# Moving six of sixteen small copies from SyncE's DMA queue to ScalarE's, in the first attention pair of an encoder block

## The chip, the cores and the metric

The kernel runs on one core of a Trainium2 chip. The metric is the device time of one execution in microseconds (us). A core has five engines that run their own instruction streams and wait for each other by semaphores: TensorE (PE in the profile) for matmuls, VectorE (DVE), ScalarE (ACT), GpSimd (POOL) and SyncE (SP). SP, ACT and POOL can also issue DMA transfers; in this kernel SP issues nearly all of them.

## The reference

Two layers on a 512 x 1024 float32 input. Layer A is dilated sliding-window attention, layer B a 2-D neighbourhood attention. Cut to layer A's core:

```
hn   = rms_norm(x)
proj = hn @ w_in                       # q, k, v of three dilation groups, and a gate
for g, dilation in ((0, 1), (1, 4), (2, 16)):
    q, k = rms_norm(q_g), rms_norm(k_g)          # per head, 16 heads of 64
    logits = q @ k.T * scale + t5_bias           # only keys within the window
    p = exp(logits - max); denom = sum(p)
    out_g, lse_g = (p @ v) / denom, max + log(denom)
y = sum over g of softmax(lse)_g * out_g         # merged by denominators
x = x + (y * silu(gate)) @ w_out
```

## The kernel before, in words

Layer A works on its 16 heads in eight pairs, `hc` 0 to 7. All large products are done in three passes of float32r halves (`mm3`: high by high, high by low, low by high), so each weight block that comes from memory (`wraw`) is first cast by ACT to its high half (`wh`, in `cast`, L157) and then subtracted by POOL or DVE to its low half (`wl`, in `rest`, L162). Casts run five to six weight blocks ahead of the matmuls that use them.

TensorE's order is written by hand. Two generators are interleaved: `main` (L1378) yields after each `mm3` of the large products; `side` (L1390) holds the attention of the pair that was projected last. `run` (L1142) steps `main` and, in between, lets `side` go on when a planned time is over. That time is `clock`, which only `matmul` and `transpose` move (L320 to L328): a step of `mm3` on 512 columns counts 640 units. `later_on(delay, job)` (L344) writes a job of another engine at the first step whose clock has passed the delay; `yield "wait", key, delay` holds `side` until `stamp[key]` plus the delay. These numbers set the order in which instructions are written, for PE, and from the first pair on also for the other engines, whose instructions of layer A are kept in program order; on the chip each waits only for its semaphores.

The attention of a pair is `attn_a` (L938). `scores(u)`, twice, writes the logits of two tiles of 128 queries by two heads. For each of these four, `least` adds the bias and takes the minimum on DVE, `exponents` and `normalise` run on ACT, and `turn` transposes the 128 x 512 block of probabilities in 32 x 32 blocks on DVE into `pq` (shown as `pt`). For the two dilated groups `pq` is then in place. For the undilated group the 32-row blocks have to change partitions: `move(n)` (L954) copies, for four (n, b), 32 partitions x 512 elements (64 KB) from `pq` to `t0` (also shown as `pt`) by DMA: sixteen copies for a pair. When all are written, `stamp["pt", hc]` is set.

Then `v_a` (L789) transposes the values `vt` on PE (`tp`) and copies them with ACT to `v`; `weigh` (L1037) multiplies probabilities by values into four `o` banks: two groups of 64 matmuls on `pq` and `rawk`, then 64 on `t0` and `v`, with steps of the large products in between; `weighed` (L851) multiplies the gate `gt` by `o` on DVE. The next pair's bias `e` is loaded by `bias_a` (L874) from SP, six loads; in the first pair behind `weigh`, in later ones ahead of it. Meanwhile `main` ends the pair's own projection: `v0_a(0)` (L673) with its `vt` copies on ACT, then the last product (`put21`, L724, whose squares of `rawk` run on ACT), and the next pair's first product.

In the first pair the sixteen moves are written on SP at delays 8000, 9300, 10600 and 11900 behind the second scores, four at a time.

Of the kernel before, what the change touches and what calls it, by code (L numbers as in the profile page):

```python
# [26 lines left out]
NHC = 8  # L27
# [19 lines left out]
def tile_hybrid_encoder(  # L47
# [49 lines left out]
    vec, act, pol, syn = (Ordered(e) for e in (nc.vector, nc.scalar, nc.gpsimd, nc.sync))  # L97
# [246 lines left out]
    def later_on(delay, job):  # L344

        timers.append((clock[0] + delay, job))
        timers.sort(key=lambda t: t[0])
# [441 lines left out]
    def v_a(hc):  # L789

        yield "wait", ("vt", hc), 2500
        vt = st.pop(("vt", hc))
        tp = bank("tp")
        for i in range(4):
            transpose(tp[:, i * P : (i + 1) * P], vt[:, i * P : (i + 1) * P])
        st["v0"] = wk.tile([P, 2, 4, P], F32, tag="k12", name="v0", bufs=1)[:, 0]
        act.copy(st["v0"], tp.rearrange("p (i c) -> p i c", i=4))
        yield
# [75 lines left out]
    def bias_a(hc):  # L874
        e0 = wk.tile([P, 2, 256], F32, tag="e0", name="e0", bufs=1)
        e12 = wk.tile([P, 4, 224], F32, tag="e12", name="e12", bufs=1)
        for hd in range(2):
            h = 2 * hc + hd
            syn.dma_start(
                e0[:, hd, :],  # L880
                bass.AP(l0_d.tensor, l0_d.offset + h * 1600 + 127, [[400, 4], [-4, 32], [1, 256]]),
            )
            for g in range(2):
                syn.dma_start(
                    e12[:, 2 * hd + g, :],
                    bass.AP(l12_d.tensor, l12_d.offset + h * 512 + 256 * g + 31, [[0, 4], [-1, 32], [1, 224]]),
                )
        return e0, e12
# [49 lines left out]
    def attn_a(hc):  # L938
# [6 lines left out]
        moved = []  # L945
# [5 lines left out]
            src = pr[:, 512 - P * n : 512]  # L951
            vec.transpose(dst, src.rearrange("p (i b k) -> p i b k", b=4, k=32))

        def move(n):  # L954

            place = t0.rearrange("p (a x) -> p a x", a=4)
            for b in range(4):
                a = (b + n) % 4
                src = pq[32 * a : 32 * a + 32, 1024 * b : 1024 * b + 512]
                tc.keep_in_program_order(syn.dma_start(place[32 * b : 32 * b + 32, a, :], src))  # L960
            moved.append(n)
            if len(moved) == 4:
                stamp["pt", hc] = clock[0]

        def scores(u):

            tiles = []
            for t in (2 * u, 2 * u + 1):
                cs, n = (64, 192) if t == 0 else (0, 192) if t == 3 else (0, 256)
                tiles.append((t, [bank("log") for _ in range(2)], cs, n))  # L970
            for t, lgs, cs, n in tiles:
                ks = slice(P * t + cs, P * t + cs + n)
                qs = slice(P * t, P * t + P)
                mm3_heads(
                    [lg[:, cs : cs + n] for lg in lgs],
                    lambda hs: q0h[hs, qs], lambda hs: q0l[hs, qs],
                    lambda hs: k0h[hs, ks], lambda hs: k0l[hs, ks], False,
                )
            for t, lgs, cs, n in tiles:
                for g in range(2):  # L980
                    for j in range(4):
                        c = P * t + 32 * j
                        for hd in range(2):
                            hs = slice(64 * hd, 64 * hd + 64)
                            matmul(
                                lgs[hd][32 * j : 32 * j + 32, 256 + P * g : 384 + P * g],
                                q12[hs, g, c : c + 32],
                                by_class(k12[hs, g, :])[:, :, j],
                                share=2,
                                start=False,  # L990
                                stop=(g == 1),
                            )
            return [(hd, t, lgs[hd], cs, n) for t, lgs, cs, n in tiles for hd in range(2)]
# [68 lines left out]
        if last:  # L1062
# [21 lines left out]
            for c in range(4):  # L1084
                src = gt.rearrange("p (t ja x) -> p x ja t", t=4, ja=8)[:, 4 * c : 4 * c + 4]
# [15 lines left out]
        for u in range(2):  # L1101
            for n, tile_ in enumerate(scores(u)):
                later_on(400 + 900 * n, partial(least, n, tile_))
            if u:
                stamp["scored", hc] = 0
                for n in range(4):
                    later_on(8000 + (2000 if hc else 1300) * n, partial(move, n))
            yield 8500
        fill = bias_rows() if hc == 2 else None
        yield from v_a(hc)  # L1110
        yield "wait", ("pt", hc), 2500
        if hc:
            st["e", hc + 1] = bias_a(hc + 1)
        yield "wait", ("pt", hc), (4500, 11500)[hc] if hc < 2 else 9000 if hc == NHC - 2 else 7500
        yield "wait", ("gate", hc), 4000
        gt = weighed(hc, (yield from weigh()))
        if not hc:
# [272 lines left out]
    def side():  # L1390
# [17 lines left out]
        for hc in range(NHC):  # L1408
            yield from k_a(hc)
            yield from attn_a(hc)  # L1410
# [109 lines left out]
```

## Time and profile before

| | us |
|---|---|
| Median of three runs | 858.39 |
| Lowest and highest | 854.2 and 860.99 |
| The profiled execution | 856.92 |
| Its span, first to last instruction | 855.1 |

The page of the profile gives the engines' busy time and the costliest groups; further views of the same trace list instructions in order of time (start, length, engine, line, operation, output and inputs, and in brackets the idle time ahead of it with what ended it), waits, the chain of work that ended last, the rows of one tile, and busy time by stretch. Nearly all rows have L85 or L324, the lines of the helpers that record an operation and a matmul, so rows are told apart by tile names. SPq, ACTq and POOLq are DMA issues. A wait for several semaphores is put down to the one that came last by the trace.

### The profile page before, as it was taken

Reading aid. Unit: us, or ns where it says so; the run is one execution under the profiler, and the core shown is the slowest. Engines: PE = TensorE matmul, PEld = TensorE weight load, DVE = VectorE, ACT = ScalarE, POOL = GpSimd, SP = SyncE. Lnnn points to the kernel's source line nnn. Section 1 sums busy time; section 2 is a strip of 40 time slices with the busy share of each in tenths; the row PEclk is TensorE's granted clock in tenths of the full one; section 3 lists DMA queues with packets and bytes.
Section 4 is the critical chain, followed back from the end, with each engine's and each line's share of the span. In section 5 each row is a group of like instructions: output and inputs, shape, how many; then the busy total and the mean of one; then the engine's idle time right before and its main releaser. Section 6 shows DMA issues by size and latency. Waiting matters only on the chain.

```text
span 855.1 us, 18125 instructions
## 1 busy us (share of the span) xinstructions
PE 833.6 (97%) x6611; PEld 688.8 (81%) x6611; DVE 634.5 (74%) x1653; ACT 507.5 (59%) x1066; POOL 296.5 (35%) x259
## 2 busy tenths in 40 slices
PE   9998989999999999999999999899999999999998
PEld 6876867878877878878877877689998898889786
DVE  7899895797897787786886866656578666776742
ACT  7566665765855846846846828545456654665440
POOL 5045442362453543543533514113123322322301
PEclk9999999999999999999999999999999999999999
DMA  9425754766676775776675664283264456534212
GB/s 339 138 56 134 206 130 136 144 164 193 136 174 193 159 176 180 161 164 184 157 174 178 126 193 144 80 297 112 81 193 145 124 169 185 158 134 126 84 50 99
DMA packets 56169, 131.97 MB, mean 154 GB/s; under 512 B 7184, under 2 KB 24528, under 8 KB 55952
## 3 DMA queue, kind: packets, MB, share of 16 engines
q1 hardware_dynamic: 49744, 108.78, 40.5%
q0 software_dynamic: 6048, 22.02, 15.0%
q8 instruction: 52, 0.85, 0.4%
q14 instruction: 37, 0.30, 0.1%
q10 hardware_dynamic: 288, 0.01, 0.0%
HBM read 111.73 MB, written 11.72 MB: 144 GB/s over the span
## 4 chain that ended last, share of the span: by engine, by line
PE 70%; ACT 10%; DVE 10%; DMA 5%; issue 3%; SPq 1%; POOL 1%; ACTq 0%; DVEq 0%
PE acc L324 58%; ACT p L85 4%; PE log L324 4%; PE o L324 4%; DMA wraw<-in_w 3%; PE tp L328 3%; DVE wl L85 2%; ACT wh L85 2%; SPq L85 1%; ACT rawk L85 1%; DVE rawq L85 1%; DVE na L85 1%; DMA e<-l_d 1%; DVE p L85 1%; DVE gt L85 1%
## 5 line engine op out<-in xcount | busy, mean ns | idle before, releaser
L85 POOL TENSOR_TENSOR wl<-wraw,wh 128x512 fp32r<-128x512 f32 (+1 forms) x153 | 197.4, 1291 | 425.2 <-PE acc L324 200.2
L85 ACT CAST wh<-wraw 128x512 fp32r<-128x512 f32 (+1 forms) x360 | 209.7, 593 | 198.9 <-PE acc L324 158.2
L85 DVE TENSOR_TENSOR wl<-wraw,wh 128x512 fp32r<-128x512 f32 (+1 forms) x207 | 160.4, 778 | 43.3 <-PE acc L324 33.9
L324 PE MATMUL acc<-wh,hn_h 128*128 128x384 f32 (+1 forms) x488 | 186.7, 383 | 3.0 <-DVE gt L85 1.7
L324 PE MATMUL acc<-wl,hn_h 128*128 128x384 f32 (+1 forms) x488 | 177.5, 364 | 0.4 <-DVE wl L85 0.4
L324 PE MATMUL acc<-wh,hn_l 128*128 128x384 f32 (+1 forms) x488 | 177.5, 364 | 0.0
L85 ACT ACTIVATE p<-p,mn 128x256 f32<-128x256 f32 (+2 forms) x248 | 137.7, 584 | 32.1 <-DVE mn L85 32.1
L324 PEld LDWEIGHTS acc<-wh,hn_h 128*128 128x128 f32 x488 | 92.3, 189 | 21.6 <-issue 6.8
L324 PEld LDWEIGHTS acc<-wh,hn_l 128*128 128x128 f32 x488 | 92.1, 189 | 9.8
L324 PEld LDWEIGHTS acc<-wl,hn_h 128*128 128x128 f32 x488 | 92.6, 190 | 8.5 <-DVE wl L85 1.1
L324 PE MATMUL acc<-wl,mix_h 128*128 128x512 f32 x224 | 88.2, 394 | 2.1 <-DVE wl L85 2.1
L324 PE MATMUL acc<-wh,mix_h 128*128 128x512 f32 x224 | 89.5, 400 | 0.0
L324 PE MATMUL acc<-wh,mix_l 128*128 128x512 f32 x224 | 87.8, 392 | 0.0
L324 PE MATMUL acc<-hn_h,wh 128*128 128x512 f32 x192 | 79.0, 412 | 0.3 <-ACT rawb L85 0.2
L324 PE MATMUL acc<-hn_h,wl 128*128 128x512 f32 x192 | 75.1, 391 | 0.0
L324 PE MATMUL acc<-hn_l,wh 128*128 128x512 f32 x192 | 75.0, 391 | 0.0
L85 DVE STREAM_TRANSPOSE pt<-p 128x512 f32<-128x512 f32 (+1 forms) x60 | 40.6, 687 | 23.7 <-ACT p L85 23.6
L85 DVE TENSOR_REDUCE ss<-sq 128x4 f32<-128x256 f32 (+1 forms) x96 | 46.1, 500 | 11.1 <-POOL sq L85 5.9
L324 PE MATMUL acc<-y_h,wh 128*128 128x512 f32 x128 | 51.9, 405 | 0.5 <-ACT gt L85 0.5
L324 PEld LDWEIGHTS acc<-wl,mix_h 128*128 128x128 f32 x224 | 42.3, 189 | 11.5 <-DVE wl L85 3.3
L324 PEld LDWEIGHTS acc<-wh,mix_h 128*128 128x128 f32 x224 | 42.2, 188 | 10.0 <-issue 1.6
L324 PE MATMUL acc<-y_h,wl 128*128 128x512 f32 x128 | 50.0, 391 | 0.0
(149 smaller groups left out, 1379.8 us busy)
## 6 DMA issues: line engine op xcount, KB each, us to landing
wraw<-in_w SPq DMA_DIRECT2D x95, 512.0 KB
wraw<-in_w POOLq DMA_DIRECT2D x42, 512.0 KB, 7.0
wraw<-in_w SPq DMA_DIRECT2D x38, 384.0 KB
pt<-pt SPq DMA_DIRECT2D x112, 64.0 KB
td<-tr SPq DMA_DIRECT2D x24, 224.0 KB
pt<-td SPq DMA_DIRECT2D x24, 224.0 KB
e<-l_d SPq DMA_DIRECT2D x32, 112.0 KB
e<-l_d SPq DMA_DIRECT2D x16, 128.0 KB
```

The source lines that it names most:

```text
L85: m = f(*args, **kw)
L324: nc.tensor.matmul(o, l, r, **kw)
L328: nc.tensor.transpose(o, i, ident)
```

## The change

In the first pair (`hc` 0), ten of the sixteen moves stay on SP's queue and six are issued on ACT's. The six are single moves, written one by one at delays 12000 to 16500; the ten on SP are written at 8000, 9000, 10000 and 11000. The stamp is set when all sixteen are written, so the two waits behind it, 2500 and 4500 before, are 0 in the first pair. The other pairs keep their sixteen moves on SP, their delays and their waits.

```diff
-        def move(n):
+        def move(n, queue, bs):
 
             place = t0.rearrange("p (a x) -> p a x", a=4)
-            for b in range(4):
+            for b in bs:
                 a = (b + n) % 4
                 src = pq[32 * a : 32 * a + 32, 1024 * b : 1024 * b + 512]
-                tc.keep_in_program_order(syn.dma_start(place[32 * b : 32 * b + 32, a, :], src))
-            moved.append(n)
-            if len(moved) == 4:
+                tc.keep_in_program_order(queue.dma_start(place[32 * b : 32 * b + 32, a, :], src))
+                moved.append(a)
+            if len(moved) == 16:
                 stamp["pt", hc] = clock[0]
+
+        def moves():
+            if hc:
+                for n in range(4):
+                    later_on(8000 + 2000 * n, partial(move, n, syn, range(4)))
+                return
+            for n in range(4):
+                later_on(8000 + 1000 * n, partial(move, n, syn, (0, 2, 3) if n % 2 else (1, 3)))
+            for i, (n, b) in enumerate(((0, 0), (0, 2), (1, 1), (2, 0), (2, 2), (3, 1))):
+                later_on(12000 + 900 * i, partial(move, n, act, (b,)))
...
             if u:
                 stamp["scored", hc] = 0
-                for n in range(4):
-                    later_on(8000 + (2000 if hc else 1300) * n, partial(move, n))
+                moves()
...
-        yield "wait", ("pt", hc), 2500
+        yield "wait", ("pt", hc), 2500 if hc else 0
         if hc:
             st["e", hc + 1] = bias_a(hc + 1)
-        yield "wait", ("pt", hc), (4500, 11500)[hc] if hc < 2 else 9000 if hc == NHC - 2 else 7500
+        yield "wait", ("pt", hc), (0, 11500)[hc] if hc < 2 else 9000 if hc == NHC - 2 else 7500
```

## The prediction

> **What bounds the kernel now.** I read the page's head first, to see which engine has no slack, then the waits of the stretch that the edit touches.
>
> ```profile
> span 855.1 us, 18125 instructions
> PE 833.6 (97%) x6611; PEld 688.8 (81%) x6611; DVE 634.5 (74%) x1653; ACT 507.5 (59%) x1066; POOL 296.5 (35%) x259
> PE o L324 <- DMA e<-l_d: 2.8, 1, 2.8
> PE o L324 <- DMA pt<-pt: 1.0, 1, 1.0
> ```
>
> PE is busy for 97%, so only its idle time and its slow matmuls are to be had. The waits of 104 to 134 us put 3.8 us of idle PE ahead of the matmuls into `o`, on DMAs. The first is put down to `e<-l_d`, but those matmuls read `pt` and `v` and no `e`: a shared landing, misread. PE's timeline there, and the same group in the next pair, where nothing waits:
>
> ```profile
> 125.28 0.39 PE L324 MATMUL acc<-wh,hn_l 128*128 128x512 f32 x1
> 128.50 0.59 PE L324 MATMUL o<-pt,v 128*64 128x64 f32 x8 [2.83 <-DMA e<-l_d]
> 130.06 3.06 PE L324 MATMUL o<-pt,v 128*64 128x64 f32 x56 [0.97 <-DMA pt<-pt]
> 133.06 0.80 PE L324 MATMUL acc<-wh,hn_h 128*128 128x512 f32 x1
> 193.56 2.08 PE L324 MATMUL o<-pt,v 128*64 128x64 f32 x64
> 195.57 0.50 PE L324 MATMUL acc<-wh,hn_h 128*128 128x512 f32 x1
> ```
>
> PE runs dry at 125.67 (125.28 + 0.39) and is back on `acc` at 133.06: 7.39 us. In the next pair the same 64 matmuls take 2.01 (193.56 to 195.57). So the stall costs 5.4 us here, of which 3.8 is idle and 1.6 slow matmuls (the granted clock below). What it waits for, by the chain, by SP's timeline and by the rows of `pt`:
>
> ```profile
> 112.77 0.70 DVE L85 STREAM_TRANSPOSE pt<-p 128x512 f32<-128x512 f32 x1
> 113.50 11.74 SPq L85 DMA_DIRECT2D pt<-pt  x16
> L85 SPq DMA_DIRECT2D pt<-pt x16: 515/591/1458, 113.5 to 124.6; - x16
> 124.63 5.39 DMA pt<-pt
> 125.36 0.50 SPq L85 DMA_DIRECT2D wraw<-in_w  x1
> 125.91 6.67 SPq L85 DMA_DIRECT2D e<-l_d  x6
> ```
>
> The last transpose ends at 113.47; SP issues 16 moves one after another until 125.24 (11.74/16 = 0.73 us each); the sixteenth starts at 124.63 and has landed 5.39 us later, at 130.02, when PE goes on. Is SP's issuing the limit, or the transfer? DMA by stretches of 2 us (length, granted clock, share, GB/s):
>
> ```profile
> 116.00:118.00 2.00, 1.00 0.43 106
> 118.00:120.00 2.00, 1.00 0.32 80
> 122.00:124.00 2.00, 1.00 0.81 131
> 126.00:128.00 2.00, 1.00 1.06 223
> 130.00:132.00 2.00, 0.58 0.50 189
> 132.00:134.00 2.00, 0.56 0.20 55
> ```
>
> While SP issues moves alone, the DMA engines are a third busy: the issue is the limit. Only from 122 do they fill, with POOL's accumulating loads, `wraw` and `e`. The last two rows show the clock halved just behind the stall.
>
> **The change, part by part.** *Moved, not removed:* the same 16 transfers of 64 KB; six issue on ACT, ten stay on SP. Order from the code: the planner counts 640 units for three matmuls. The six fire at 12160, 13440, 14080, 14720, 15796 and 17076; the copy of `vt` is written at 12160, just behind the first. `weigh` was due at 17076 and, with the waits now zero behind the last move, is due there again: PE's order does not change.
>
> *SP:* ten moves at 0.73 us from 113.50 end at 120.8 (at 0.63, the usual spacing without its two long ones, 119.8). Its last starts near 120.1; with the same 5.39 us it has landed by 125.5. Behind it the `wraw` load and six `e` loads go out some 4.5 us earlier; `e` is free (its readers are the minima of the scores) and nobody waits for it before the next scores.
>
> *ACT:* what its queue holds there:
>
> ```profile
> 113.49 0.60 ACT L85 CAST wh<-wraw 128x512 fp32r<-128x512 f32 x1
> 114.00 1.05 ACT L85 COPY vt<-acc 128x512 f32<-128x512 f32 x1
> 115.08 0.24 ACT L85 COPY vt<-vt 128x64 f32<-128x64 f32 x1
> 116.28 0.58 ACT L85 COPY v<-tp 128x512 f32<-128x512 f32 x1
> 116.75 1.33 ACT L85 CAST wh<-wraw 128x512 fp32r<-128x512 f32 x2
> 124.04 0.42 ACT L85 ACTIVATE sq<-rawk 128x256 f32<-128x256 f32 x1 [5.96 <-DVE rawk L85]
> 0.74 0.41 ACTq L85 DMA_DIRECT2D ng<-in_norm_gain  x1
> 1.18 0.46 ACTq L85 DMA_DIRECT2D hg<-in_head_gain  x1
> 1.18 4.10 DMA hg<-in_head_gain
> 115.38 0.65 PE L328 MATMUL tp<-ident,vt 128*128 128x128 f32 x4 [0.24 <-ACT vt L85]
> ```
>
> The wait for the last transpose (113.47) is over when ACT arrives at 114.0, so the first move adds no wait, only its issue. Price of one issue on ACT: no row shows a move there. Nearest below, 0.41 (`ng` at 0.74); above, SP's longest move, 1.46; I take SP's median, 0.59, the same transfer. Six cost 3.5 us (2.5 to 8.8). ACT was idle for 5.96 us from 118.08 to 124.04, so 3.5 is hidden: its last move starts near 121.0 and is out by 121.6. Queued behind the moves are four casts of `wh`, up to 3.5 us late; who waits for them:
>
> ```profile
> 121.26 1.59 POOL L85 TENSOR_TENSOR wl<-wraw,wh 128x512 fp32r<-128x512 f32 x1
> 124.53 0.68 DVE L85 TENSOR_TENSOR wl<-wraw,wh 128x512 fp32r<-128x512 f32 x1
> ```
>
> These two subtract the last two casts (casts are used in order), at 121.26 and 124.53, and the casts would end by 119.9 and 121.0: hidden. If an issue cost 1.46, the last cast would end near 125.2, still ahead of its matmuls at 129.7, but the sixth move would not start before 125.4.
>
> What isn't hidden: the first move stands ahead of the `vt` copy, and PE already waits 0.24 us for that copy ahead of `tp`. **Price: one issue, +0.6** (bounds: 0, if ACT's sequencer issues while the cast at 113.49 still runs; 1.46).
>
> *The landing:* PE now comes to the last 64 matmuls at 126.3 (125.67 + 0.6). The sixth ACT move starts at 121.0; from issue to landing the rows give 4.10 (`hg`, on this queue) and 5.39 (above), and the page's median for POOL's 512 KB loads is 7.0:
>
> ```profile
> wraw<-in_w POOLq DMA_DIRECT2D x42, 512.0 KB, 7.0
> ```
>
> That is 125.1, 126.4 or 128.0: a wait of 0 to 1.7 us, by the middle row 0.1. I take 0.1, since 5.39 was measured on a move in full DMA engines, which it will meet again.
>
> *Rules weighed.* The Trainium skill, "DMA: Bandwidth & Descriptors", section "Issuing engines are not separate DMA queues", says that several issuing engines share the same 16 DMA engines and save only the initiating time, usually small beside the transfer. The shares of 0.32 and 0.43 above speak for issue as the limit; by the rule the landing stays at 130 and the sum is 0 (rival B, from rows).
>
> *What is late next.* DVE multiplies `gt` by `o` after its own chain, and PE's next transposes need the banks that this frees:
>
> ```profile
> 130.54 0.42 DVE L85 TENSOR_TENSOR rawk<-rawk,rs 128x256 f32<-128x256 f32 x1
> 132.54 0.93 DVE L85 TENSOR_TENSOR gt<-gt,o 128x128 f32<-128x128 f32 x4 [1.58 <-PE o L324]
> 136.91 0.60 PE L328 MATMUL tp<-ident,rawq 128*128 128x128 f32 x4
> 133.00:194.00 61.00, 60.81 (x542) 48.79 (x540) 47.29 (x112) 40.54 (x79) 26.95 (x22) 0.99 0.63 145
> ```
>
> With `o` done at 128.4, DVE comes to it at 130.96 and frees the first bank at 131.2; PE reaches `tp` at 128.4 + 3.5 = 131.9. That fits by 0.7 us. Behind 133 PE is busy for 60.81 of 61 us (first number after the length), so what is saved is passed on.
>
> *Sum:* −5.4 (stall and slow matmuls) −0.3 (the first `acc` step took 0.80 us at the low clock, 0.50 in the next pair) +0.6 +0.1 = **−5.0 us**. The profiled execution took 856.92 (span 855.1): it becomes 851.9. The median of the three runs is 858.39, 1.5 above: 853.4 there, which I give.
>
> **The rivals.**
>
> *A, part of the wait stays.* `wraw` and `e` are pulled forward into the landing of ACT's moves, beside POOL's loads. With the 7.0 us landing PE waits 1.7 instead of 0.1, and at the upper issue price a little more: −2 to −3.4, about 855.7 on the median. For: the share of 1.06 at 126. Against: ACT's moves stand on a queue of their own, not behind SP's. Whether so short a wait halves the clock too, no row here shows; I price it without. The rows of 130 to 134 show the clock halved behind 3.8 us of idle; the Trainium skill, "TensorE: Matmul & The Clock Gate", section "Part 1: The HAM clock gate", gives an idle window of about 3.4 us as what throttles it, which agrees, and by which 1.7 us would cost only itself.
>
> *B, nothing saved: the transfer is the limit, or the change doesn't do what it says.* Either the moves land no earlier, or the sixth falls behind the square of `rawk`, which stood until 124.04. It would start at 124.5, land at 129.9, and PE goes on at 130.06 as before; the 0.6 ahead of `tp` only shortens the wait. That is 858.4, no change. Against: the shares, and the planner's 17076 for the move, 800 ahead of the square.
>
> *C, slower: ACT's issue is dear.* It decides from about 1.4 us for each. ACT then ends its sixth move at about 126.9 (118.08 + 8.8), started at 125.4, landed at 130.8; PE loses 1.46 ahead of `tp`, comes at 127.1, waits 3.7, and goes on at 130.8 instead of 130.06, at the low clock: +0.7, and six times the excess of whatever an issue takes beyond 1.46: 859.1, 860 at 1.6. For: SP has such rows (1458 ns). Against: its median is 591.
>
> **Chances and range.** The forecast 0.62, A 0.18, B 0.12, C 0.05; 0.03 for a knock-on later in the kernel, of either sign. Runs before spread from 854.2 to 860.99, so 1% (8.6 us) is about what a measurement here tells from no change. The whole stall is 5.7 us, 0.66%: faster by over 1% needs luck or a knock-on, 0.08; slower by over 1% 0.03; within, 0.89. Range: from no loss ahead of `tp` with a low median (−7, and the spread of the runs), 848.5, to C at 860, which takes in B.
>
> **What would show it.** Right: ten moves on SP, gone by 121; six on ACT between 113.5 and 121.6 at about 0.6 each; `tp` from `vt` idle for about 0.8; the last 64 matmuls at about 126.3, within 2.1 us, at a clock of 1.00 from 130 to 134; `gt` times `o` at 131. Wrong: an idle PE ahead of these matmuls of over 2 us (A, B), an ACT issue over 1.2 (C), a sixth move behind the square (B), or a new wait behind 133 that takes the gain back.

## The result, and the profile after

The changed kernel took 850.86 us (median of 8 runs, 849.09 to 852.54) against 858.38 for the kernel before beside it (8 runs): a ratio of 0.9923 [0.9896, 0.995]. That is −7.5 us. A second comparison gave 851.66 against 856.49: 0.9945 [0.9929, 0.996], or −4.8 us. The forecast was −5.0 us. Both ratios are less than 1% below 1, and neither interval takes in 1. The profiled execution took 849.09 us, with a span of 847.1.

The head of the page, then SP's timeline and PE's around the last 64 matmuls (start, length, engine, line, operation, output and inputs, idle time ahead):

```profile
span 847.1 us, 18124 instructions
PE 828.3 (98%) x6611; PEld 684.4 (81%) x6611; DVE 634.2 (75%) x1653; ACT 507.8 (60%) x1066; POOL 297.4 (35%) x259
```

```profile
112.66 6.77 SPq L85 DMA_DIRECT2D pt<-pt  x10
119.56 0.50 SPq L85 DMA_DIRECT2D wraw<-in_w  x1
120.10 10.63 SPq L85 DMA_DIRECT2D e<-l_d  x6
...
114.71 0.65 PE L328 MATMUL tp<-ident,vt 128*128 128x128 f32 x4 [0.86 <-ACT vt L85]
...
124.53 0.39 PE L324 MATMUL acc<-wh,hn_l 128*128 128x512 f32 x1
124.85 2.08 PE L324 MATMUL o<-pt,v 128*64 128x64 f32 x64
126.87 0.50 PE L324 MATMUL acc<-wh,hn_h 128*128 128x512 f32 x1
...
130.41 0.60 PE L328 MATMUL tp<-ident,rawq 128*128 128x128 f32 x4
```

The 64 matmuls stand in one row now, of 2.08 us, with no idle time in brackets; before they were two rows with 2.83 and 0.97 ahead. From the end of the last `acc` step (124.92) to the next (126.87) PE spends 1.95 us, where it spent 7.39. Ten moves leave SP in 6.77 us. The other six, on ACT's timeline, stand between its casts (`wh`) and copies in the order of the working (some rows are left out at the dots, here as elsewhere):

```profile
112.66 0.61 ACT L85 CAST wh<-wraw 128x512 fp32r<-128x512 f32 x1
112.67 0.61 ACTq L85 DMA_DIRECT2D pt<-pt  x1
113.32 1.06 ACT L85 COPY vt<-acc 128x512 f32<-128x512 f32 x1
...
114.42 0.51 ACTq L85 DMA_DIRECT2D pt<-pt  x1
...
116.99 0.78 ACTq L85 DMA_DIRECT2D pt<-pt  x1
117.28 0.62 ACT L85 CAST wh<-wraw 128x512 fp32r<-128x512 f32 x1
123.14 0.42 ACT L85 ACTIVATE sq<-rawk 128x256 f32<-128x256 f32 x1 [5.24 <-DVE rawk L85]
```

The rows of the tile `pt` give the issues (lowest, median and highest length in ns, first and last start):

```profile
L85 SPq DMA_DIRECT2D pt<-pt x10: 523/590/666, 112.7 to 118.8; - x10
L85 ACTq DMA_DIRECT2D pt<-pt x6: 514/579/779, 112.7 to 117.0; - x6
```

The DMA view of 112 to 119 says which packets of ACT's queue, q10, began there (packets, MB, share of the engines):

```profile
q10 hardware_dynamic: 288, 0.39, 23.3%
```

And two stretches (start and end, length, busy time of PE, PEld, DVE, ACT and POOL, granted clock, DMA share, GB/s):

```profile
126.00:128.00 2.00, 2.00 (x38) 1.76 (x34) 1.79 (x7) 0.13 (x1) 0.77 (x1) 1.00 0.94 201
128.00:130.00 2.00, 2.00 (x11) 1.64 (x10) 1.86 (x8) 1.56 (x3) 0.00 (x0) 1.00 0.50 100
```

Six moves of 64 KB are 0.39 MB: all packets of ACT's six had begun by 119. The trace also records each semaphore increment of a DMA; by these the last of the six had landed at 119.25, 2.3 us behind its start at 116.99, and PE came for them at 124.85. The clock stays at 1.00.

**Where the 8.0 us of these two spans are.** PE's instructions stand in the same order in both traces, so one row of before can be set against its own of after. `tp` from `vt` starts at 115.38 before and 114.71 after: −0.67 was there ahead of the stall. `tp` from `rawq` starts at 136.91 and 130.41: −6.50. So the stall itself gave −5.83, and another −1.5 came behind it. The first part is the clock of another stretch, 82 to 86, halved before and whole after, behind a wait for `wl` that both traces have; part of the last is two waits that only the trace before has. The waits of 76 to 84, the same row in both:

```profile
PE acc L324 <- DVE wl L85: 2.1, 1, 2.1
```

The stretch 82 to 86 before:

```profile
82.00:86.00 4.00, 4.00 (x20) 2.95 (x21) 3.88 (x6) 2.52 (x5) 2.29 (x4) 0.57 0.97 184
```

and after:

```profile
82.00:86.00 4.00, 4.00 (x87) 3.01 (x86) 3.93 (x6) 2.59 (x5) 2.30 (x4) 1.00 0.95 171
```

The two waits, in PE's timeline of before:

```profile
272.42 0.38 PE L324 MATMUL log<-k0h,q0h 64*128 64x256 f32 x1 [0.69 <-ACT k L85]
459.87 0.39 PE L324 MATMUL log<-k0h,q0h 64*128 64x256 f32 x1 [0.48 <-ACT k L85]
```

The experiments show that these change from one execution to the next of one kernel: the second trace of the changed kernel has the first of the two waits again, at 268 (0.72 us).

### The profile page after: what moved, and what is told of

It reads as the page before. It is cut to its first block, busy times and chain, and to the rows that moved or that the text cites. A ratio compares the mean times of both kernels' runs of the same rounds, so it can differ in the third digit from the quotient of the medians.

```text
span 847.1 us, 18124 instructions
## 1 busy us (share of the span) xinstructions
PE 828.3 (98%) x6611; PEld 684.4 (81%) x6611; DVE 634.2 (75%) x1653; ACT 507.8 (60%) x1066; POOL 297.4 (35%) x259
## 4 chain that ended last, share of the span: by engine, by line
PE 74%; ACT 9%; DVE 9%; DMA 4%; issue 3%; POOL 1%; SPq 1%; DVEq 0%; ACTq 0%
PE acc L324 61%; PE log L324 5%; PE o L324 4%; ACT p L85 4%; PE tp L328 3%; DMA wraw<-in_w 2%; DVE wl L85 2%; ACT wh L85 2%; ACT rawk L85 1%; DVE na L85 1%; DVE rawq L85 1%; DMA e<-l_d 1%; DMA pt<-in_xt 1%; DVE p L85 1%; DVE gt L85 1%
```

## The experiments

Two questions were open. What made the last moves late: the length of SP's queue alone, the waits and stamps that the edit changed with it, or what the transfers met on the way? And is the difference of 2.5 us between the first result and the forecast a gain or chance? In the diffs of the moves, `-` is the changed kernel. Ratios are to the kernel before, with 95% intervals.

### Both kernels again: how much is chance

No edit in either.

> The kernel before, run again, for a second profiled execution. Theory P (the stall is in the program): PE is idle for 3 to 4.5 us ahead of the last 64 matmuls of the first weigh group, as in the first profile, and the ratio is 1.00 within 0.4%. Theory C (chance: the first profile showed an unlucky execution): the stall is below 2 us here. For the granted clock behind the stalls at 78 and 126 us: if the halving is a matter of when a window falls, one of the two places may show a full clock this time (worth 1.0 us at 82 and 1.6 to 2.0 us at 130).

> The changed kernel, run again. The first comparison took 7.5 us off the median where 5.0 were forecast. Theory P (the extra 2.5 us belong to the change): ratio 0.991 again, and the offset behind the third and sixth pair grows again by about 1.6 us against the kernel before. Theory C (chance of the clock and of DMA timing): the ratio lies between 0.991 and 0.995, and in the two second profiles the offset from the first pair's weigh to the end differs from the first one's by 1 us or more.

Measured: 1.0001 [0.9985, 1.0018] for the kernel before and 0.9945 [0.9929, 0.996] for the changed one. PE's timeline of the kernel before again has the stall (`issue` in brackets: the view names no releaser; by the increments two moves land at 127.23 and 127.45, just ahead of 127.54):

```profile
127.54 0.71 PE L324 MATMUL o<-pt,v 128*64 128x64 f32 x8 [2.91 <-issue]
128.49 2.97 PE L324 MATMUL o<-pt,v 128*64 128x64 f32 x56 [0.24 <-DMA pt<-pt]
```

and that of the changed kernel again has not:

```profile
126.73 2.08 PE L324 MATMUL o<-pt,v 128*64 128x64 f32 x64
```

Yet the spans are 851.6 for the kernel before (855.1 in the first profile) and 851.2 for the changed one (847.1). Two profiles of one kernel differ by about 4 us, as much as the change is worth: single spans can't size it. In the second profile of the changed kernel the clock of 82 to 86 was 0.61, in the second of the kernel before it was 1.00, the other way round than in the first pair. The stall stands in both profiles of the kernel before and in neither of the changed one. The 2.5 us by which the first result passed the forecast lie within what executions of one kernel differ by, and the two intervals overlap.

### The six moves back on SP, with the new waits

```diff
-                later_on(12000 + 900 * i, partial(move, n, act, (b,)))
+                later_on(12000 + 900 * i, partial(move, n, syn, (b,)))
```

> As the change (its delays, its zero waits, the same places in PE's order), but the six moves issued on SP too. Theory I (SP's serial issue is the limit): SP is busy with sixteen moves until about 10.5 to 11.7 us behind the last transpose, PE is idle for 3 to 4.5 us ahead of the last 64 matmuls, ratio 0.998 to 1.002. Theory W (the new delays and waits bring the gain, not the second queue): ratio 0.991 to 0.993, no stall.

Measured: 1.0038 [1.0021, 1.0054], slower than expected by either theory. The rows of `pt`:

```profile
L85 SPq DMA_DIRECT2D pt<-pt x16: 514/590/1684, 112.4 to 123.8; - x16
```

The timeline, SP's row and PE's:

```profile
112.40 11.96 SPq L85 DMA_DIRECT2D pt<-pt  x16
...
129.65 3.69 PE L324 MATMUL o<-pt,v 128*64 128x64 f32 x64 [5.09 <-DMA pt<-pt]
133.26 0.80 PE L324 MATMUL acc<-wh,hn_h 128*128 128x512 f32 x1
```

The new waits and stamps save nothing without the second queue: the stall is back and larger, 5.09 us idle in one piece and the matmuls at half clock. Why it is larger than before (whose sixteen go out in another order) stays open.

### Two moves on ACT, and four

```diff
-                later_on(8000 + 1000 * n, partial(move, n, syn, (0, 2, 3) if n % 2 else (1, 3)))
-            for i, (n, b) in enumerate(((0, 0), (0, 2), (1, 1), (2, 0), (2, 2), (3, 1))):
+                later_on(8000 + 1000 * n, partial(move, n, syn, range(4) if n % 2 else (0, 1, 3)[n == 0 :] + (2,) * (n == 0)))
+            for i, (n, b) in enumerate(((0, 0), (2, 2))):
                 later_on(12000 + 900 * i, partial(move, n, act, (b,)))
+            later_on(16500, lambda: stamp.update({("pt", hc): clock[0]}))
```

With four, the list is (0, 0), (1, 1), (2, 2), (3, 1). The last line sets the stamp where the sixth move sets it in the changed kernel, so that PE's order stays.

> As the change, with two moves on ACT and fourteen on SP; PE's order is unchanged. SP issues its last at about 8.5 us behind the first, near 121.5, and PE comes to the last 64 matmuls near 124.9 to 125.7. Theory I (issue alone; a move lands about 2 us behind its issue, as ACT's did): landed by 123.5 to 124, no stall, ratio 0.991 to 0.993 like the change. Theory T (what counts is to be ahead of POOL's accumulating loads, which start at 120 to 121; behind them a move takes 5.4 us): landed near 126.5 to 127, a stall of 1 to 2 us, ratio 0.994 to 0.997.

Measured with two: 0.9983 [0.9971, 0.9995], less gain than either theory gave. SP's row of `pt`:

```profile
L85 SPq DMA_DIRECT2D pt<-pt x14: 523/591/1314, 112.5 to 121.4; - x14
```

The timeline of POOL and PE:

```profile
119.63 0.88 POOL L85 DMA_DIRECT2D wraw<-in_w  x1 [3.20 <-PE acc L324]
...
126.15 0.34 PE L324 MATMUL o<-pt,v 128*64 128x64 f32 x4 [1.34 <-issue]
127.66 3.52 PE L324 MATMUL o<-pt,v 128*64 128x64 f32 x60 [1.18 <-DMA pt<-pt]
```

and the stretch behind the wait:

```profile
128.00:130.00 2.00, 2.00 (x41) 2.00 (x40) 1.84 (x6) 0.00 (x0) 0.00 (x0) 0.50 0.79 172
```

SP's last move starts 8.9 us behind its first, where it was 11.1 in the kernel before, and PE gets it at 127.66: 6.2 us behind its start at 121.4, where ACT's last in the changed kernel landed in 2.3. A transfer of 64 KB that takes almost three times as long isn't held up by its issue. POOL's load of `wraw` went out at 119.63: by the increments, the moves issued up to 119.50 landed 2.0 to 2.3 us behind their start, the three behind the load 5.9 to 6.8. And 2.5 us of idle in two pieces went with a halved clock, so the stall kept its second part.

> The change with four moves on ACT and twelve on SP; PE's order is the same. SP's last is issued near 120.5 to 121.5 on a stretch that starts at 113, within a microsecond of GpSimd's first accumulating load. Theory T: it stands between the six (no stall) and the two (2.5 us): landed between 123 and 126, a stall of 0 to 1.2 us, no halved clock, ratio 0.993 to 0.997.

> Four moves on ACT once more. The first time its profile had no stall in the first pair, like the change, but its median lay 1.9 us below the kernel before instead of 4.8, and its profiled execution lost 2.8 us in the seventh pair, where PE waits for a late block of weights by way of ACT. Theory C (that loss comes and goes with the timing of the loads): ratio 0.994 to 0.997 and another place or size of the late loss. Theory S (with four on ACT the loads fall so that the loss is regular): ratio 0.997 to 0.999 and the loss in the same pair again.

Measured with four: 0.9977 [0.9956, 0.9998], and again 0.9978 [0.9958, 0.9998]. In the first trace the stall is gone (`o` takes 2.09 us without a wait), in the second 0.73 us of it are left. In both, only SP's last move stands behind POOL's load, by 0.3 and 0.6 us; by the increments it takes 4.3 and 5.6 us to land, all the others about 2. Yet more than half of the gain is missing in both measurements. In both traces PE waits for `k` at the logits of a later pair. The waits of 446 to 468 in the first:

```profile
PE log L324 <- ACT k L85: 2.1, 2, 1.3
```

The second has 1.4 us there, and neither trace of the changed kernel has any. The loss came twice at one place, which speaks for a pattern; but one trace of the kernel before has 0.48 us there and that of all_on_sp 0.7, so two traces do not prove it. Whether this wait is the whole of the missing gain, and what links four moves to a pair that comes 320 us later, stays open.

### Without POOL's loads, and with them later

Behind the first pair's moves POOL issues two loads of `wraw` that add a second weight block to one already in place (`self.add`), for pair 2. Two kernels leave them out, one from the version with two moves on ACT and one from the kernel before; a third, again the kernel before with all sixteen moves on SP and nothing left out, issues them later:

```diff
-                self.add(j + 3 + 2 * i, b11[i], b12[i].off)
+                b11[i].used(j + 3 + 2 * i) if hc == 2 else self.add(j + 3 + 2 * i, b11[i], b12[i].off)
```

```diff
-                self.add(j + 3 + 2 * i, b11[i], b12[i].off)
+                self.add(j + 8 + i if hc == 2 else j + 3 + 2 * i, b11[i], b12[i].off)
```

> Two moves on ACT, fourteen on SP, and GpSimd's two accumulating loads of the third pair's first weight block (512 KB each, issued 7 and 10 us behind the first move) left out, so that part of the third pair's product is computed from other weights. Theory T (the last moves land late because they meet those loads): with the loads gone a move lands about 2 us behind its issue, as ACT's six did: the last, issued near 121.4, by 124; the stall ahead of the last 64 matmuls, 2.5 us with the loads, falls below 0.5, the clock stays whole, ratio 0.993 to 0.996. Theory L (a queue of fourteen is slow by itself, whatever else runs): the stall stays at 2 us or more, ratio 0.998.

> The kernel before, all sixteen moves on SP, with the same two accumulating loads left out. Theory T: the last move, issued near 124, lands 2 to 3 us later instead of 5.4: the stall falls from 3.8 to about 1 us and the clock stays whole, ratio 0.995 to 0.998; what is left of the stall is then the issue's own share. Theory L: stall 3 us or more, ratio 1.00.

> The kernel before, whole, all sixteen moves on SP; only the two accumulating loads of the third pair are written five and three and a half weight blocks' turns later, so that GpSimd issues them near 126 and 128 instead of 120.5 and 124, behind the last move. Theory T (those loads make the last moves land late): the last move, issued near 124, lands about 2.5 to 3.5 us later; the stall ahead of the last 64 matmuls falls from 3.8 to about 1 us, the clock stays whole, ratio 0.994 to 0.997 with no second queue at all. Theory I (SP's serial issue alone): the stall stays at 3 us or more, ratio 1.00. A price may come behind: the sums that read these blocks could wait.

Measured: 0.993 [0.9907, 0.9954] with two moves on ACT and no loads; 0.9953 [0.9932, 0.9974] for the kernel before without them; 0.9951 [0.9932, 0.9971] for the kernel before with the loads late. With two moves on ACT and no loads, PE has no wait ahead of the last 64 matmuls:

```profile
125.97 2.08 PE L324 MATMUL o<-pt,v 128*64 128x64 f32 x64
```

The kernel before without the loads, its row of `pt`:

```profile
L85 SPq DMA_DIRECT2D pt<-pt x16: 514/590/772, 113.6 to 123.8; - x16
```

and PE's timeline:

```profile
127.31 2.08 PE L324 MATMUL o<-pt,v 128*64 128x64 f32 x60 [0.19 <-DMA e<-l_d]
```

With the loads late, the row of `pt`:

```profile
L85 SPq DMA_DIRECT2D pt<-pt x16: 523/590/684, 112.5 to 122.5; - x16
```

and the timeline of POOL and PE:

```profile
124.89 0.87 POOL L85 DMA_DIRECT2D wraw<-in_w  x1
126.92 1.00 POOL L85 DMA_DIRECT2D wraw<-in_w  x1
...
125.69 2.08 PE L324 MATMUL o<-pt,v 128*64 128x64 f32 x64
```

This shows the cause. With all sixteen moves on one queue and no loads the last starts as late as 123.8, but PE goes on 3.5 us later instead of 5.4, and 0.2 us of the stall is left. With the whole computation and the loads moved to 124.89, no stall is left, and the gain is that of the change (0.9951 and 0.9945, with intervals that overlap). Even the long issue rows go: the longest is 684 ns, against 1458 in the kernel before.

Two ends are open. In these three kernels PE waits 0.6 to 0.8 us for `wl` some 5 us ahead of the 64 matmuls, which it does not in the kernel before; it comes that much later, so without this wait up to about 0.8 us of the stall (an estimate from these rows) would still show. And without POOL's loads the last two of sixteen moves still take 4.0 and 3.7 us by the increments, with all the others at about 2; why was not found.

### How ACT pays: six ahead of the copies, none ahead, ten in all

```diff
-                later_on(12000 + 900 * i, partial(move, n, act, (b,)))
+                later_on(12000, partial(move, n, act, (b,)))           # six_ahead_of_vt
+                later_on(12200 + 850 * i, partial(move, n, act, (b,))) # first_behind_vt
+                later_on(12000 + 500 * i, partial(move, n, act, (b,))) # ten_on_act, ten in the list
```

The names behind `#` are those of the three kernels. six_ahead_of_vt also sets the stamp at 16500, as with two moves; in ten_on_act SP keeps the other six.

> The change with all six moves written on ACT ahead of the copy of vt; PE's order is the same. Theory O (a DMA issue holds ACT's next instruction for its 0.6 us, and only what ACT has already begun runs beside it): the copy of vt starts near 116.2 instead of 113.3, PE is idle for 3 to 4 us ahead of the transposes of vt, and with a halved clock behind it the gain of the change is nearly gone: ratio 0.997 to 1.001. Theory F (issues cost ACT nothing, as the change's first one seemed to: 0.15 us): the idle time stays near 0.8 us, ratio 0.994.

Measured: 0.9991 [0.9962, 1.002]. The gain is lost. The timeline of ACT and PE:

```profile
113.74 4.39 ACTq L85 DMA_DIRECT2D pt<-pt  x6
118.17 1.08 ACT L85 COPY vt<-acc 128x512 f32<-128x512 f32 x1 [3.84 <-DMA pt<-pt]
...
119.58 0.66 PE L328 MATMUL tp<-ident,vt 128*128 128x128 f32 x4 [4.21 <-ACT vt L85]
```

and the stretch behind it:

```profile
120.00:122.00 2.00, 2.00 (x8) 1.62 (x7) 1.79 (x2) 1.57 (x4) 1.57 (x2) 0.55 0.44 107
```

From the end of its cast on ACT does nothing while its queue issues six moves. The copies of `vt` come 3.84 us late, PE waits 4.21, and the clock falls to 0.55: the stall has only changed its place.

> The change with the first of ACT's six moves written behind the copies of vt instead of ahead of them. By the trace of the change ACT's vt copies end 0.15 us later for that move; PE's wait ahead of the transposes of vt falls by 0.1 to 0.6 us, and the rest is as in the change: ratio 0.993 to 0.995, not to be told from the change.

Measured: 0.9946 [0.9924, 0.9967]. With all six behind the copies, PE still waits 0.64 us for `vt` ahead of `tp` (0.86 in the changed kernel). The 0.2 us that this should save can't be told from nothing.

> The change with ten moves on ACT, 500 units apart, and six on SP. ACT's last issue ends near 120.5, still ahead of the square of rawk that waits until 123 to 124; the casts between are 2 to 3 us later than with six. Theory O with the cover found in the profile (5 us of idle ACT): no stall, ratio 0.993 to 0.996 like the change. Theory D (late casts reach PE through the low halves): new waits of PE on wl within 15 us, ratio 0.996 or more.

Measured: 0.9952 [0.9928, 0.9977], with a stall of 0.9 us that had not been expected. ACT's row of `pt`:

```profile
L85 ACTq DMA_DIRECT2D pt<-pt x10: 522/602/807, 113.7 to 121.0; - x10
```

and PE's timeline:

```profile
126.69 0.45 PE L324 MATMUL o<-pt,v 128*64 128x64 f32 x8
128.05 1.85 PE L324 MATMUL o<-pt,v 128*64 128x64 f32 x56 [0.90 <-DMA pt<-pt]
```

Here it is ACT's last move, at 121.0, that PE gets 7 us later. It stands behind POOL's load (120.82), but that is not all. With only six moves of its own, SP comes early to its next loads, which only copy; SP's timeline, and what the queues of SP (q1) and ACT (q10) began from 120 to 122:

```profile
118.68 0.50 SPq L85 DMA_DIRECT2D wraw<-in_w  x1
q1 hardware_dynamic: 120, 0.47, 76.3%
q10 hardware_dynamic: 24, 0.04, 5.5%
```

ACT's moves at 118.66, 119.53 and 120.14 are out ahead of POOL's load, of which no packet begins before 122, and still take 4.7 to 5.8 us by the increments, while SP's queue is busy with `wraw` and then `e`. So a load that only copies holds moves up as well. Neither the queue of a move nor POOL's adding decides here, but whether the move is out ahead of the large loads, whichever queue they are on. None of these versions beats the change by more than the runs can tell.

## Why the prediction was right, and which terms were not

**Right.** The stall was there in both traces of before and is in neither of after: −5.83 between the two `tp` rows, where the working had 5.7 for the stall and the first `acc` step. It is passed on to the end: −7.5 by the first comparison and −4.8 by the second, −5.0 forecast. The order in ACT's queue is the one worked out, an issue costs 579 ns there (0.59 taken), the casts behind the moves end at 117.9 and hide, and ten moves take SP 6.77 us (7.3 and, with the usual spacing, 6.3). `gt` times `o` comes at 129.99, ahead of PE's `tp` at 130.41, so nothing new is late there. None of the rivals came about. That the sum came so close is in part luck: of its two small terms, 0.1 was nothing and 0.6 came about for another reason, as the next paragraphs show.

**The landing** was the term that was wrong. The working gave ACT's last move a start at 121.0 and 5.39 us to land, and PE a wait of 0.1. It started at 116.99, since the casts and copies run beside the issues and not between them, and it had landed 2.3 us later; PE came 5.6 us behind that. SP's tenth started at 118.8 and took 2.0 us by the increments. 5.39 is the price of a move that goes out behind a large load, and the change brings its moves out ahead of it. POOL's timeline before, and then after:

```profile
120.65 0.88 POOL L85 DMA_DIRECT2D wraw<-in_w  x1 [3.43 <-PE acc L324]
123.95 0.88 POOL L85 DMA_DIRECT2D wraw<-in_w  x1 [1.10 <-DVE wl L85]
119.75 0.88 POOL L85 DMA_DIRECT2D wraw<-in_w  x1 [3.20 <-PE acc L324]
```

The trace of before had this in it. By the increments, its eleven moves that start up to 120.59 land 1.9 to 2.4 us later, and the five behind POOL's load at 120.65 take 4.6 to 5.9. The reading "the issue is the limit" of the stretches of 116 to 120 was thus half of the cause. Slow issuing puts the last moves behind the load, and the load makes them late. The working saw the DMA engines full from 122 on, but took for granted that ACT's moves would meet them so again; it did not ask whether a move that is out sooner lands sooner.

**Ahead of `tp`** the idle time is 0.86 as foretold (0.8), but not for the reason given. From the start of the cast to `tp` it is 1.89 us before (113.49 to 115.38) and 2.05 after (112.66 to 114.71): the first issue runs beside the cast already started and costs 0.16 of the 0.6, near the lower bound that had been named. With no move ahead of the copies (first_behind_vt) the idle time was still 0.64, and in the second trace of the kernel before it was 0.67. The other 0.45 is PE's: its last `acc` step ahead of `tp` ends 1.65 us behind the start of that cast before and 1.20 after, so PE came earlier and waited longer. That the 0.8 was met is luck.

**Rival A's price** for a short wait left the clock whole. Two moves on ACT show 2.5 us of idle in two pieces and a halved clock behind them (0.50 in 128 to 130), so that most of the gain is lost; 0.9 us, with ten, left it whole. The Trainium skill, "TensorE: Matmul & The Clock Gate", section "Part 1: The HAM clock gate", was read there as saying that an idle stretch below about 3.4 us costs only itself. These runs do not bear that out: 1.34 and 1.18 us in separate rows were enough once, and behind the wait of 2.1 us at 81 the clock was 0.57 in one execution of the kernel before and 1.00 in another. Even the 3.8 us of the kernel before, which the prediction took as agreeing, were two pieces of 2.83 and 0.97.

**The other rule weighed**, of the Trainium skill, "DMA: Bandwidth & Descriptors", section "Issuing engines are not separate DMA queues", agrees with the runs in that the DMA engines are shared: with ten on ACT, its moves were held up behind SP's and POOL's loads. That the initiating time is small beside the transfer holds for one move here (0.59 us to issue, about 2 to land), but not for sixteen in a row, which took SP 11.74 us: that time decided which moves got out ahead of the load, and was worth the whole stall.

## What to carry to other kernels

When a chain of small DMAs ends late, look at two rows: the start of the last one, and the large transfer that any queue, its own or another, issued shortly ahead of it. Splitting the chain over two queues and moving the large transfer back by 4 to 5 us gave the same gain here, and the second needs no new work on a compute engine. Where DMAs go on a compute engine's queue, write them one at a time between other instructions and not in a row ahead of what the critical engine waits for: here six in a row left PE waiting for 4.21 us, where the first of the change, alone, delayed the copies by 0.16.

## What the runs showed of the hardware that was not expected

- A move of 64 KB landed about 2 us behind its start (1.9 to 2.5 by the increments of the two kernels' first traces) when it was out ahead of the 512 KB loads. PE got the last one 5.4, 5.9 and 6.2 us behind its start when it went out after POOL's load (kernel before, all on SP, two on ACT). With ten on ACT, moves that went out with or behind SP's plain load at 118.68 took 4.7 to 5.8 us, and the last, behind POOL's as well, 7.
- An issue on ACT runs beside an instruction that has already started (0.16 us of delay for one), but holds the next one: six in a row took 4.39 us, and PE waited 4.21.
- The clock halves after idle times that differ from run to run: behind 2.1 us at 81, 0.57 in one execution and 1.00 in another; behind 2.5 us in two pieces, 0.50.
